# The first tile's clip and store in one piece instead of two, in a contrast adjustment on one Trainium2 core

## The chip, the cores and the metric

The kernel runs on one core of a Trainium2 chip. The core has five engines with their own instruction streams: TensorE (PE), VectorE (DVE), ScalarE (ACT), GpSimd (POOL) and SyncE (SP). Data moves between the chip's main memory and the on-chip memory (128 partitions) by DMA. A DMA is issued by an engine's queue, here SP for loads and ACT for stores, and is carried out row by row by the core's 16 DMA engines. The metric is the device time of one execution in microseconds, given as the median of several runs.

## The reference

The input is `x`, 16 x 3 images of 512 x 512 float32, and a factor of 1.5:

```python
def reference(x, factor):
    mean = np.mean(x, axis=(2, 3), keepdims=True)
    return np.clip(mean + factor * (x - mean), 0, 1).astype(np.float32)
```

Each of the 48 images needs its own mean before any of its pixels can be written. Input and output are 50.33 MB each.

## The kernel before

The 48 images are laid end to end and cut into rows of `ROW` = 8192 elements (32 KB). An image is 32 rows, so a tile of 128 partitions holds four whole images, 4 MiB, and there are 12 tiles. The on-chip buffer `ring` has `BUFS` = 6 slots of one tile each; tile t lives in slot t % 6 from its load to the end of its store, and is changed in place.

`load` (L76, issued by SP) fetches a tile or a part of its columns. At the start five loads are issued with nothing to wait for: the first 2048 columns of tile 0 (`SHORT`), its other 6144 columns, tile 1, tiles 2 and 3 in one DMA, tiles 4 and 5 in one DMA. These fill all six slots. Load t + 6 is issued after the work on tile t is written down, and waits until the store of tile t has landed, as it overwrites the same slot.

`compute(t)` sums the tile in two parts: VectorE adds up the first 4352 columns (L81) and ScalarE the other 3840 (L84, an activation that copies into `junk` and accumulates). Two small matmuls with the block matrix `blockw` (L86, L87) add the sums of the 32 rows of an image and scale them, so that `bias` (PSUM) holds (1 - factor) x mean for each row. VectorE then makes two passes over the tile: x * factor + bias (L91), and the clip to [0, 1] (L94). ACT issues the store (L101). For tile 0 alone the two passes and the store are done for 2048 columns first and then for the other 6144 (`FIRST`), so that this tile has four passes and two stores, with rows of 8 KB and of 24 KB; all other tiles have two passes and one store of 32 KB rows.

The order is written by hand: in each engine's stream the instructions of tile t stand before those of tile t + 1. So ACT's activation for tile t + 1 stands behind the store of tile t, and VectorE's sum of tile t + 1 behind the clip of tile t. Waits on semaphores are put in by the framework from what each instruction reads and writes.

Of the kernel before, what the change touches and what calls it, by code (L numbers as in the profile page):

```python
# [1 line left out]

# [4 lines left out]


P = 128  # L10
ROW = 8192
BUFS = 6
SHORT = 2048
FIRST = (SHORT, ROW - SHORT)
SUM = 4352


@with_exitstack
def kernel(
    ctx: ExitStack,  # L20
    tc: tile.TileContext,
    x: bass.AP,
    factor: float,
    out: bass.AP,
):

    nc = tc.nc
    f32 = mybir.dt.float32  # L30
    Alu = mybir.AluOpType
    Act = mybir.ActivationFunctionType

    B, C, H, W = x.shape
    n_img, n_pix = B * C, H * W
    ppi = n_pix // ROW
    per_tile = P // ppi
    n_tiles = n_img // per_tile
    assert ppi * ROW == n_pix and per_tile * n_tiles == n_img

    factor = float(factor)
    wconst = (1.0 - factor) / float(n_pix)

    x_f = x.rearrange("b c h w -> (b c h w)")
    out_f = out.rearrange("b c h w -> (b c h w)")

    def dram(ap, t, c0=0, c1=ROW):
        return bass.AP(tensor=ap.tensor, offset=t * P * ROW + c0, ap=[[ROW, P], [1, c1 - c0]])

    consts = ctx.enter_context(tc.tile_pool(name="consts", bufs=1))  # L50
    xpool = ctx.enter_context(tc.tile_pool(name="xpool", bufs=1))
    small = ctx.enter_context(tc.tile_pool(name="small", bufs=1))
    psum = ctx.enter_context(tc.tile_pool(name="psum", bufs=1, space=bass.MemoryType.PSUM))


    sums = small.tile([P, 2 * n_tiles], f32, name="sums")
    junk = small.tile([P, ROW - SUM], f32, name="junk")
    bias = psum.tile([P, n_tiles], f32, name="bias")

    blockw = consts.tile([P, P], f32, name="blockw")  # L60
    nc.gpsimd.memset(blockw, 0.0)  # L61
    for a in range(0, P, ppi):
        nc.gpsimd.memset(blockw[a : a + ppi, a : a + ppi], wconst)  # L63


    ring = xpool.tile([P, BUFS, ROW], f32, name="ring")

    def load(t, c0=0, c1=ROW, n=1):

        b = t % BUFS  # L70
        src = bass.AP(
            tensor=x_f.tensor,
            offset=t * P * ROW + c0,
            ap=[[ROW, P], [P * ROW, n], [1, c1 - c0]],
        )
        nc.sync.dma_start(out=ring[:, b : b + n, c0:c1], in_=src)  # L76

    def compute(t):
        xt = ring[:, t % BUFS, :]
        own = sums[:, 2 * t : 2 * t + 2]  # L80
        nc.vector.tensor_reduce(  # L81
            out=own[:, 0:1], in_=xt[:, 0:SUM], axis=mybir.AxisListType.X, op=Alu.add
        )
        nc.scalar.activation(out=junk, in_=xt[:, SUM:ROW], func=Act.Copy, accum_out=own[:, 1:2])  # L84
        shift = bias[:, t : t + 1]
        nc.tensor.matmul(shift, blockw, own[:, 1:2], start=True, stop=False)  # L86
        nc.tensor.matmul(shift, blockw, own[:, 0:1], start=False, stop=True)  # L87
        c = 0
        for n in FIRST if t == 0 else [ROW]:
            part = xt[:, c : c + n]  # L90
            nc.vector.tensor_scalar(  # L91
                out=part, in0=part, scalar1=factor, scalar2=shift, op0=Alu.mult, op1=Alu.add
            )
            nc.vector.tensor_scalar(  # L94
                out=part, in0=part, scalar1=0.0, scalar2=1.0, op0=Alu.max, op1=Alu.min
            )
            store(t, c, c + n)
            c += n

    def store(t, c0, c1):  # L100
        nc.scalar.dma_start(out=dram(out_f, t, c0, c1), in_=ring[:, t % BUFS, c0:c1])  # L101

    with tc.manual_schedule():
        load(0, c1=SHORT)
        load(0, c0=SHORT)
        load(1)
        load(2, n=2)
        load(4, n=2)
        for t in range(n_tiles):
            compute(t)  # L110
            if t + BUFS < n_tiles:
                load(t + BUFS)


# [1 line left out]
_INS = ['x', 'factor']  # L116
_OUTS = [((16, 3, 512, 512), 'float32')]

_NUMBERS = {'factor': 1.5}


# [26 lines left out]
```

## Time and profile before

| what | value |
|---|---|
| median of 3 runs | 239.26 us (239.2 to 239.46) |
| span of the profiled execution | 237.3 us |
| moved by DMA | 100.66 MB, mean 424 GB/s over the span |
| loads | 50.33 MB in 11 DMAs, issued by SP |
| stores | 50.33 MB in 13 DMAs, issued by ACT |
| VectorE busy | 163.1 us |
| ScalarE busy | 43.2 us |
| one sum on VectorE (L81) | 4.68 us |
| one whole-tile pass, L91 / L94 | 4.49 / 4.43 us |

The span reaches from the first to the last instruction of one profiled execution; the time of a run is some 2 us more, for what lies around it. The DMA line of the profile gives for each of 40 slices how busy the 16 DMA engines were, in tenths. A packet in the queue lists is one row of a transfer, or one of the tiny writes that signal a completion. The queue lists can be asked for any stretch of time; packets are counted in the stretch in which they begin, so that a short stretch can show more than 100%.

### The profile page before, as it was taken

How to read it: one execution, taken by the hardware profiler on the slowest of the kernel's cores; microseconds unless marked ns; L12 is line 12 of the kernel's file. 1: busy time of each engine (PE TensorE's matmuls, PEld its weight loads, DVE VectorE, ACT ScalarE, POOL GpSimd, SP SyncE). 2: the span in 40 equal slices, each digit the busy share in tenths (PEclk: the TensorE clock that was granted, in tenths of full speed). 3: DMA queues.
4: the chain of work that ended last, by engine and by line, in shares of the span. 5: the costliest groups of instructions: out<-in, count | busy, mean ns of one | idle time of the engine just before them, and what ended most of it. 6: DMA issues, size and time to landing. Idle time of an engine off the chain costs nothing.

```text
span 237.3 us, 285 instructions
## 1 busy us (share of the span) xinstructions
PE 14.1 (6%) x48; PEld 12.0 (5%) x48; DVE 163.1 (69%) x38; ACT 43.2 (18%) x25; POOL 0.9 (0%) x9
## 2 busy tenths in 40 slices
PE   0010010001010001010010100100100100010000
PEld 0010010001010001010010100100100100010000
DVE  0079989048989328999989898891892795687000
ACT  2050230041050023050320504101400500500000
POOL 1000000000000000000000000000000000000000
DMA  7999999999999999999999999999999999999996
GB/s 297 410 442 442 421 442 359 456 439 441 442 436 414 403 431 442 442 442 442 436 442 436 414 409 425 442 442 442 442 436 442 436 420 403 425 442 442 442 442 265
DMA packets 3712, 100.66 MB, mean 424 GB/s; under 512 B 384, under 2 KB 384, under 8 KB 384
## 3 DMA queue, kind: packets, MB, share of 16 engines
q1 hardware_dynamic: 1840, 50.33, 49.7%
q10 hardware_dynamic: 1872, 50.33, 49.2%
HBM read 50.33 MB, written 50.33 MB: 424 GB/s over the span
## 4 chain that ended last, share of the span: by engine, by line
DMA 57%; DVE 29%; another core or an unknown queue 3%; PE 1%; SPq 1%; issue 0%; DVEq 0%
DMA ring<-in_x_dram 41%; DMA out_dram<-ring 16%; DVE sums L81 10%; DVE ring L91 9%; DVE ring L94 9%; PE bias L87 1%; SPq L76 1%; DVEq L91 0%
## 5 line engine op out<-in xcount | busy, mean ns | idle before, releaser
L81 DVE TENSOR_REDUCE sums<-ring 128x1 f32<-128x4352 f32 x12 | 56.2, 4683 | 45.7 <-DMA ring<-in_x_dram 45.7
L84 ACT ACTIVATE junk<-ring 128x3840 f32<-128x3840 f32 x12 | 40.8, 3403 | 163.3 <-DMA ring<-in_x_dram 107.5
L91 DVE TENSOR_SCALAR ring<-ring,bias 128x8192 f32<-128x8192 f32 (+2 forms) x13 | 54.1, 4163 | 8.9 <-PE bias L87 7.4
L94 DVE TENSOR_SCALAR ring<-ring 128x8192 f32<-128x8192 f32 (+2 forms) x13 | 53.3, 4099 | 0.4
L86 PE MATMUL bias<-sums,blockw 128*128 128x1 f32 x24 | 7.0, 361 | 190.8 <-ACT junk L84 190.8
L86 PEld LDWEIGHTS bias<-sums,blockw 128*128 128x128 f32 x24 | 6.0, 312 | 191.7 <-ACT junk L84 175.2
L87 PE MATMUL bias<-sums,blockw 128*128 128x1 f32 x24 | 7.0, 363 | 4.3 <-DVE sums L81 3.9
L87 PEld LDWEIGHTS bias<-sums,blockw 128*128 128x128 f32 x24 | 6.0, 311 | 5.3 <-DVE sums L81 5.0
L84 ACT ACTIVATION_READ_ACCUMULATOR junk<-ring 128x1 f32 x12 | 2.2, 186 | 0.0
L84 ACT ACT_TABLE_LOAD x1 | 1.3, 1283 | 0.7 <-PEq L129 0.7
L63 POOL MEMSET blockw<- 32x32 f32 x4 | 0.5, 117 | 0.2
L61 POOL MEMSET blockw<- 128x128 f32 x1 | 0.2, 204 | 0.3 <-POOLq L129 0.3
L129 POOL MEMSET const-bfloat16-1.0<- 128x1 bf16 x1 | 0.1, 111 | 0.0
L129 POOL MEMSET const-uint8-127<- 128x1 uint8 x1 | 0.1, 111 | 0.0
L129 POOL MEMSET const-float32-1.0<- 128x1 f32 x1 | 0.1, 108 | 0.0
L129 POOL MEMSET const-float32-0.0<- 128x1 f32 x1 | 0.1, 103 | 0.2 <-issue 0.2
## 6 DMA issues: line engine op xcount, KB each, us to landing
out_dram<-ring ACTq DMA_DIRECT2D x11, 4096.0 KB, 35.8
ring<-in_x_dram SPq DMA_DIRECT2D x7, 4096.0 KB, 49.7
ring<-in_x_dram SPq DMA_DIRECT2D x2, 8192.0 KB, 66.7
ring<-in_x_dram SPq DMA_DIRECT2D x1, 3072.0 KB, 11.7
out_dram<-ring ACTq DMA_DIRECT2D x1, 3072.0 KB, 28.2
ring<-in_x_dram SPq DMA_DIRECT2D x1, 1024.0 KB, 4.8
out_dram<-ring ACTq DMA_DIRECT2D x1, 1024.0 KB, 17.5
```

The lines of the kernel that those rows point to most:

```text
L61: nc.gpsimd.memset(blockw, 0.0)
L63: nc.gpsimd.memset(blockw[a : a + ppi, a : a + ppi], wconst)
L76: nc.sync.dma_start(out=ring[:, b : b + n, c0:c1], in_=src)
L81: nc.vector.tensor_reduce(out=own[:, 0:1], in_=xt[:, 0:SUM], axis=mybir.AxisListType.X, op=Alu.add)
L84: nc.scalar.activation(out=junk, in_=xt[:, SUM:ROW], func=Act.Copy, accum_out=own[:, 1:2])
L86: nc.tensor.matmul(shift, blockw, own[:, 1:2], start=True, stop=False)
L87: nc.tensor.matmul(shift, blockw, own[:, 0:1], start=False, stop=True)
L91: nc.vector.tensor_scalar(out=part, in0=part, scalar1=factor, scalar2=shift, op0=Alu.mult, op1=Alu.add)
L94: nc.vector.tensor_scalar(out=part, in0=part, scalar1=0.0, scalar2=1.0, op0=Alu.max, op1=Alu.min)
L129: nc = _bacc.Bacc("TRN2", target_bir_lowering=False, num_devices=1)
```

## The change

Tile 0 is treated like every other tile: two passes over all 8192 columns, then one store. The constant `FIRST` and the loop over parts go. The loads stay as they are, the split first load included.

```diff
 SHORT = 2048
-FIRST = (SHORT, ROW - SHORT)
 SUM = 4352
...
         nc.tensor.matmul(shift, blockw, own[:, 0:1], start=False, stop=True)
-        c = 0
-        for n in FIRST if t == 0 else [ROW]:
-            part = xt[:, c : c + n]
-            nc.vector.tensor_scalar(
-                out=part, in0=part, scalar1=factor, scalar2=shift, op0=Alu.mult, op1=Alu.add
-            )
-            nc.vector.tensor_scalar(
-                out=part, in0=part, scalar1=0.0, scalar2=1.0, op0=Alu.max, op1=Alu.min
-            )
-            store(t, c, c + n)
-            c += n
+        nc.vector.tensor_scalar(
+            out=xt, in0=xt, scalar1=factor, scalar2=shift, op0=Alu.mult, op1=Alu.add
+        )
+        nc.vector.tensor_scalar(
+            out=xt, in0=xt, scalar1=0.0, scalar2=1.0, op0=Alu.max, op1=Alu.min
+        )
+        store(t, 0, ROW)
```

In the built program VectorE has two instructions fewer and ACT one store fewer; the order of everything else on every engine is the same. The completion semaphores of the DMAs, of which there are eight, are shared out in turn, so that with one DMA fewer some stores get another one.

## Prediction
> **What bounds the kernel now.** I read the page first: the engine shares, the line of 40 slices and the DMA queues.
>
> ```profile
> span 237.3 us, 285 instructions
> PE 14.1 (6%) x48; PEld 12.0 (5%) x48; DVE 163.1 (69%) x38; ACT 43.2 (18%) x25; POOL 0.9 (0%) x9
> DMA  7999999999999999999999999999999999999996
> q1 hardware_dynamic: 1840, 50.33, 49.7%
> q10 hardware_dynamic: 1872, 50.33, 49.2%
> ```
>
> No compute engine is full, and the DMA engines are full in every slice but the first and the last. Queue q1 carries the loads, q10 the stores. Their packets take 49.7 + 49.2 = 98.9% of 16 engines' span, 234.7 us of 237.3; the other 2.6 us are the start and the end. So the time is the sum of the packet times, and moving work earlier or later changes nothing unless it leaves the DMA engines idle or changes what a packet costs. The chain of waits gives DVE 29% of the span, which could mislead: transfers run all through those stretches.
>
> Next, the DMA queues of chosen stretches. The columns are packets, MB, and packet time as a share of 16 engines' time in the stretch. First the steady state, 60 to 200 us, where load rows and store rows of 32 KB alternate:
>
> ```profile
> q1 hardware_dynamic: 1039, 30.90, 51.1%
> q10 hardware_dynamic: 1025, 29.92, 49.5%
> ```
>
> 30.90 MB are 943 rows of 32,768 B (the other packets are tiny ones). 51.1% x 16 x 140 us / 943 = 1.214 us for a load row; the stores give 1.215 by the same division. Now 22 to 36 us, in which the first store (8 KB rows) starts to move, and then 36 to 46 us, in which the second store (24 KB rows) takes over:
>
> ```profile
> q1 hardware_dynamic: 148, 4.78, 81.1%
> q10 hardware_dynamic: 113, 0.93, 15.6%
> ...
> q1 hardware_dynamic: 79, 2.59, 65.1%
> q10 hardware_dynamic: 91, 1.60, 37.2%
> ```
>
> From 22 to 36 us the loads have 146 rows (4.78 MB / 32,768 B) and take 81.1% x 224 = 181.7 us, where 146 x 1.214 = 177.2 would do: 4.4 us too much over 16 engines, 0.28 us of time. From 36 to 46 us it is 79 rows and 65.1% x 160 = 104.2 us against 95.9: 8.3 us too much, 0.52 us of time. So load rows are slower than anywhere else just where the two odd stores begin, by 0.80 us together. The printed tenths of a per cent make these figures uncertain by about 0.02 us.
>
> Last, the start and the end in order of time:
>
> ```profile
> 19.65 1.23 DVE L94 TENSOR_SCALAR ring<-ring 128x2048 f32<-128x2048 f32 x1
> 20.79 3.42 DVE L91 TENSOR_SCALAR ring<-ring,bias 128x6144 f32<-128x6144 f32 x1
> 20.91 7.06 ACTq L101 DMA_DIRECT2D out_dram<-ring  x2
> 24.25 3.36 DVE L94 TENSOR_SCALAR ring<-ring 128x6144 f32<-128x6144 f32 x1
> ...
> 203.76 4.69 DVE L81 TENSOR_REDUCE sums<-ring 128x1 f32<-128x4352 f32 x1 [4.98 <-DMA ring<-in_x_dram]
> ...
> 218.17 0.34 ACTq L101 DMA_DIRECT2D out_dram<-ring  x1
> ```
>
> The first store is issued at 20.91 us; the queue's rows show none of it before 24.0 us and 16 of its packets, one per engine, from 24 to 26 us, so the lag from issue to first row is some 4 us while the loads are running (the first load of all, on idle engines, lags 1.0 us at most to its first bytes: issued at 0.74 us, 33 GB/s already in the first 2 us).
>
> **The change, part by part.** Four VectorE passes over tile 0 become two. Before: 1.29 + 1.23 + 3.42 + 3.36 = 9.30 us. After: 4.49 + 4.43 = 8.92 us by the rows of the other eleven tiles. The 0.3 to 0.4 us lie beside transfers: VectorE afterwards waits 8.77 us for tiles 2 and 3. Taken at nothing; without that cover it would be 0.4 us gained.
>
> One store issue goes (0.34 us on the ScalarE queue, in which the activation of tile 1 stands next); nothing waits for it. The store of tile 0 is issued at 18.33 + 4.53 + 4.46 = 27.3 us (one pass-to-pass distance and one pass-to-issue distance of a whole tile) instead of 20.91: 6.4 us later. Until its rows begin at about 31.3 us, the loads have the engines alone. That is no loss, since 24 MiB of loads are queued, 57 us of work at 437 GB/s.
>
> What is late next: the loads run ahead first and then give half to the store. Before, the stores have moved 4.23 MB by 56 us, as 8 KB and 24 KB rows get less than half beside 32 KB load rows. After, they move from 31.3 to 56 us at 433/2 GB/s: 5.3 MB, or 4.8 MB if the queue gives up one turn of 16 rows between two stores. So the stores are 0.6 to 1.1 MB ahead and the loads as much behind, and at half of 433 GB/s each later load lands 2.8 to 5.2 us later. Tile 0's slot comes free a few us before 55.96 us, where SyncE now issues load 6; its queue holds tiles 4 and 5 then, so it gains nothing.
>
> The end has to absorb this. From 204 us to the end the stores move 13.63 MB at 437 GB/s; the last tile is 4.19 MB or 9.6 us of it, so its rows begin near 226.0 us, 7.8 us after their issue at 218.17. Landing 2.8 to 5.2 us later leaves 2.6 to 5.0 us of cover. A lag of 1 us fits in any case, one of 4 us in most of it. Idle DMA time taken: nothing; bounds 0 and 1.4 us (4.0 - 2.6).
>
> The built program shares out the completion semaphores anew, so the stores of tiles 5, 6 and 7 also wait for loads 6, 7 and 8. Queued behind each on ScalarE is the activation of the next tile, which needs that load or a later step anyhow. Tile 7's store is the closest (issued at 144.88 us, load 8 in use at 145.73): about 1 us, with store 6 still in the queue to cover it. Nothing.
>
> What remains is the price of packets. (a) The odd rows themselves: 8 rows per engine of each kind. 15.6% x 224 us / 113 = 0.309 us for 8 KB; a 24 KB row, whose own row I take from the rate of the loads, is 0.91 us. Together 1.22 us against 1.214 for 32 KB, times 8: 0.06 us gained. (b) The 0.52 us at the takeover by the 24 KB rows: the takeover is gone, and every other one (60 to 200 us) shows load rows at 1.214. Gained 0.52; bounds 0 and 0.52. (c) The 0.28 us where stores first move: there is still a first store, with rows four times as long. No row of this trace shows 32 KB stores starting beside loads. Bounds: 0 (as at each later takeover) and 0.80 (all that the start now costs in two steps). I take 0.28 as the nearest row, so no change.
>
> The Trainium skill ("DMA: Bandwidth & Descriptors", section "Anatomy of one DMA") puts about 2 us of fixed cost on each DMA. One DMA fewer would by that give 237.3 us; the steady rows, with engines full while each completion is pending, say that this part is hidden. The same page's "Rules for kernel authors" wants transfers issued early, which speaks against the change: the 6.4 us later issue would by that cost up to 6.4 us, an estimate of 245.7 us, but here the engines are full of loads meanwhile.
>
> Sum: -0.06 - 0.52 = -0.58 us on the profiled 237.3. The median of the runs is 239.26, 2.0 us above it for what lies around the span, which stays: 238.7 us.
>
> **The rivals.** First, the loss belongs to the store stream's coming up to full share, and one start of 32 KB rows costs the whole 0.80 us. For it: both slow stretches stand at the beginning of the stores and none comes later. Against: the takeover from 24 to 32 KB rows near 55 us costs nothing. Only the 0.06 us remain: 239.2 us. Second, a clean start, as at all later takeovers: 0.06 + 0.80 = 0.86 us gained, 238.4 us. Third, on the other side, the last store comes too late: if the whole 6.4 us of delay reach the last load, its store is issued at 224.6 us, and with 4 us of lag its rows start at 228.6 instead of 226.0: 2.6 us of idle engines between the last two stores, 239.26 - 0.58 + 2.6 = 241.3 us. It decides from an issue after 222.0 us at that lag, after 225.0 us at a lag of 1 us. Against it: loads and stores share out the same bytes, so the loads fall behind only by what the stores gain.
>
> **How the numbers follow.** Forecast 0.46, first rival 0.28, second 0.12, third 0.14. This kernel's measurement can tell about 0.2% (0.48 us) from no change, so faster is below 238.78 us and slower above 239.74. The forecast lies close to the lower line: I count 0.36 of its 0.46 as faster and 0.10 as same. Faster 0.36 + 0.12 = 0.48; same 0.10 + 0.28 = 0.38; slower 0.14. The range takes in the forecast and the first two rivals, with 0.2 to 0.3 us for the spread of the three runs (0.26): 238.2 to 239.5 us.
>
> **What would show it.** The packet time of the loads between 36 and 46 us back at 1.214 us a row; an excess near 0.28 us around 31 us; the two queues' shares adding to about 98.9% of a shorter span; the last store issued between 221 and 224 us with no slice below 9 before the end. Wrong it would be if load rows stay 0.8 us too slow around 31 us, or if the DMA line dips near 225 us.

## The result, and the profile after

| | before | changed kernel |
|---|---|---|
| median of 11 runs | 239.22 us (239.04 to 239.6) | 240.3 us (239.5 to 241.89) |
| ratio | | 1.0048, 95% interval 1.0036 to 1.0059 |
| span, median of the runs | 237.4 us | 238.1 us |
| run time less span, median | 1.87 us | 2.19 us |

The changed kernel is slower by 1.08 us; 238.7 us was predicted. (The column before takes its last two rows from the runs of that kernel that stand beside the experiments. Ratios and medians of spans leave disturbed runs out.) Of the 1.08 us some 0.7 lie inside the span and 0.32 outside it. The page of one execution of the changed kernel begins like this:

```profile
span 238.0 us, 278 instructions
PE 14.0 (6%) x48; PEld 12.0 (5%) x48; DVE 162.8 (68%) x36; ACT 43.2 (18%) x25; POOL 0.9 (0%) x9
DMA  7999999999999999999999999999999999999996
q1 hardware_dynamic: 1840, 50.33, 49.6%
q10 hardware_dynamic: 1728, 50.33, 49.1%
```

The engines of the core do the same work as before, and the DMA engines are again full in every slice but the first and the last. The packets take 49.6 + 49.1 = 98.7% of 238.0 us, 234.9 us, against 234.7 before. A printed tenth of a per cent is 0.24 us here; added up packet by packet, the sum goes from 234.51 to 234.85 us. So the packets account for 0.34 us, about half of the 0.7 us by which the span grew in this execution. The timeline of the two ends shows that nothing was late in the way the third rival needed:

```profile
22.83 4.43 DVE L90 TENSOR_SCALAR ring<-ring 128x8192 f32<-128x8192 f32 x1
27.29 0.38 ACTq L96 DMA_DIRECT2D out_dram<-ring  x1
...
221.92 0.34 ACTq L96 DMA_DIRECT2D out_dram<-ring  x1
```

The first store is issued at 27.29 us and the last at 221.92, 3.75 us later than before, with some 14 us of DMA work still ahead.

The queue lists of the changed kernel, first 28 to 36 us, where its stores start to move, then 36 to 46 us (packets, MB, share of 16 engines' time):

```profile
q1 hardware_dynamic: 53, 1.74, 63.0%
q10 hardware_dynamic: 30, 0.98, 28.4%
...
q1 hardware_dynamic: 76, 2.49, 57.6%
q10 hardware_dynamic: 64, 2.10, 48.5%
```

From 28 to 36 us 53 load rows take 63.0% x 128 = 80.6 us, and 53 x 1.214 = 64.3 would do: 16.3 us too much, 1.02 us over 16 engines. From 36 to 46 us 76 rows take 92.2 us, 1.213 each, and nothing is lost. So the start of the stores alone now costs 1.02 us, where it cost 0.28 and the takeover 0.52 before.

Most of this is lost before any store row moves. From 28 to 32 us, and then from 32 to 36 us:

```profile
q1 hardware_dynamic: 33, 1.08, 83.4%
...
q10 hardware_dynamic: 30, 0.98, 56.9%
q1 hardware_dynamic: 20, 0.66, 42.6%
```

In the first four microseconds there are loads only, and their 33 rows take 83.4% x 64 = 53.4 us where 33 x 1.214 = 40.1 would do: 0.83 of the 1.02 us. The store is issued at 27.29 us and its first row begins at 32.1 us, so the slow load rows lie between the two.

That is not all. The same list from 140 to 190 us, store queue only, first before, then after:

```profile
q10 hardware_dynamic: 377, 11.31, 52.4%
```

```profile
q10 hardware_dynamic: 381, 10.91, 50.9%
```

Before, 11.31 MB are 345 rows of 32,768 B, and 52.4% x 800 us / 345 is 1.215 us. After, 10.91 MB are 333 rows at 1.223 us. A small loss, but from the single packets it lies on ten of the 16 engines, up to 0.43 us on one between 100 and 200 us. And the engines end apart. From 235.5 us on, before and after:

```profile
q10 hardware_dynamic: 15, 0.00, 0.4%
```

```profile
q10 hardware_dynamic: 17, 0.03, 4.2%
```

Before, only completions are left; after, a whole row still begins. By the packets the engines end between 235.47 and 236.05 us before, and between 235.65 and 236.75 us after. The span follows the last of the 16, not their mean: it is 1.2 us longer than the last end in both. The mean of the 16 ends rose by 0.36 us (235.67 to 236.03), the last end by 0.7. The last engine of the changed kernel lost 0.27 us in slow rows after 60 us; without them it would end at 236.48 us, still 0.43 us after the last one before. So in this execution the larger part comes from the start.

### The profile page after: what moved, and what is told of

Read it like the earlier page. It is cut to its first block, busy times and chain, and to the rows that moved or that the text cites. A ratio compares the mean times of both kernels' runs of the same rounds, so it can differ in the third digit from the quotient of the medians.

```text
span 238.0 us, 278 instructions
## 1 busy us (share of the span) xinstructions
PE 14.0 (6%) x48; PEld 12.0 (5%) x48; DVE 162.8 (68%) x36; ACT 43.2 (18%) x25; POOL 0.9 (0%) x9
## 3 DMA queue, kind: packets, MB, share of 16 engines
q1 hardware_dynamic: 1840, 50.33, 49.6%
q10 hardware_dynamic: 1728, 50.33, 49.1%
## 5 line engine op out<-in xcount | busy, mean ns | idle before, releaser
L87 DVE TENSOR_SCALAR ring<-ring,bias 128x8192 f32<-128x8192 f32 x12 | 53.9, 4492 | 8.9 <-PE bias L86 7.5
L90 DVE TENSOR_SCALAR ring<-ring 128x8192 f32<-128x8192 f32 x12 | 53.1, 4427 | 0.4
```

What stands on the lines that cost most here:

```text
L87: nc.vector.tensor_scalar(out=xt, in0=xt, scalar1=factor, scalar2=shift, op0=Alu.mult, op1=Alu.add)
L90: nc.vector.tensor_scalar(out=xt, in0=xt, scalar1=0.0, scalar2=1.0, op0=Alu.max, op1=Alu.min)
```

## The experiments

Three theories stood at the beginning. Theory 1: the loads stall where the rows of the store stream begin or grow, and long first rows cost more. Theory 2: the 6.4 us later start costs. Theory 3: the number of store DMAs counts. Theory 4 came out of the first four runs. The offset that it speaks of is how long after a load tile's first row a store tile's first row begins, taken from the packets' start times (the median over the 16 engines, at the store of tile 4); both streams repeat every 19.4 us. Offsets and packet times come from the one execution of each kernel that was profiled, medians of spans from all its runs.

**late_two_stores.** Whole passes, but two stores:

```diff
-        store(t, 0, ROW)
+        c = 0
+        for n in (SHORT, ROW - SHORT) if t == 0 else [ROW]:
+            store(t, c, c + n)
+            c += n
```

> Two whole passes over tile 0 as in the changed kernel, and behind them two stores as in the kernel before: 8 KB rows, then 24 KB rows, both issued at about 27.3 us. Theory 1 (loads stall where the rows of the store stream begin or grow, the more the longer the new row): the loads' excess is 0.28 + 0.52 = 0.8 us again, only later, in place of 1.02 us in the changed kernel, no row is slow from 100 to 200 us, and the time is 239.2 to 239.4 us. Theory 2 (the 6.4 us later start of the stores costs): 240.3 us as in the changed kernel. Theory 3 (the number of store DMAs counts, not their rows): 239.2 us.

Measured 240.19 us, ratio 1.0034 (1.0024 to 1.0043). Theory 3 falls: the stores are as many as before and as long, and the time is near the changed kernel's. Theory 1 is not enough: the loads' excess between 20 and 60 us is 0.93 us against 0.88 before, by the packets. But rows between 100 and 160 us are slow, 0.11 us in the mean and up to 0.33 us on single engines, which theory 1 did not expect.

**early_passes_one_store.** Four passes, one store:

```diff
-            store(t, c, c + n)
             c += n
+        store(t, 0, ROW)
```

> Four passes over tile 0 as before, and one store of 32 KB rows behind them, issued at about 27.6 us. All three theories expect the time of the changed kernel, 240.0 to 240.5 us, with about 1 us of excess in the loads near 30 us; if the passes themselves mattered it would be 239.2 us.

Measured 241.11 us, ratio 1.0071 (1.0048 to 1.0094): as slow as the changed kernel or slower. The passes are not the cause.

**late_half_partitions.** Two stores of 64 partitions:

```diff
-        store(t, 0, ROW)
+        if t == 0:
+            for p in (0, P // 2):
+                half = bass.AP(tensor=out_f.tensor, offset=p * ROW, ap=[[ROW, P // 2], [1, ROW]])
+                nc.scalar.dma_start(out=half, in_=ring[p : p + P // 2, 0, :])
+        else:
+            store(t, 0, ROW)
```

> As the changed kernel, but tile 0 is stored in two DMAs of 64 partitions each, both with rows of 32 KB. Theory 1 (row length at the start): 240.3 us, about 1 us of excess near 30 us. Theory 2 (late start): 240.3 us. Theory 3 (number of store DMAs): 239.2 us.

Measured 245.94 us, ratio 1.0279. No theory expected this. By the packets 2.05 us of excess lie between 60 and 200 us, where the kernel before has 0.01, and the engines end between 238.3 and 242.5 us. Its offset is 2.7 us.

**two_halves_16k.**

```diff
-FIRST = (SHORT, ROW - SHORT)
+FIRST = (4096, 4096)
```

> The kernel before with the parts of tile 0 at 4096 and 4096 columns: first store rows of 16 KB, issued at about 23 us, and then no growth until the 32 KB rows of tile 1. Theory 1: 0.5 us of excess in the loads at the start (half of 1.02), 0 to 0.5 us where the 32 KB rows take over, so 239.0 to 239.5 us. Theory 2 (cost by the start's delay, 1.08 us for 6.4 us): the start is some 2.2 us later than before, 239.6 us. Theory 3: 239.2 us.

Measured 239.22 us, ratio 1.0 (0.9991 to 1.0008). The excess is 0.81 us, as before (0.88), though the rows start at 16 KB: what the start costs in all depends little on how the first store is cut. That a start 2 us later costs nothing speaks against theory 2.

In these runs and the two kernels of the study, slow late rows went with an offset of 1.2 us (changed kernel, late_two_stores, early_passes_one_store) or 2.7 us, and none were seen at 9.7 us (before) and 12.1 us (two_halves_16k). This is theory 4.

**later_store.** The store of tile 0 written behind ScalarE's activation of tile 1:

```diff
         nc.scalar.activation(out=junk, in_=xt[:, SUM:ROW], func=Act.Copy, accum_out=own[:, 1:2])
+        if t == 1:
+            store(0, 0, ROW)
+            load(BUFS)
...
-        store(t, 0, ROW)
+        if t:
+            store(t, 0, ROW)
...
-            if t + BUFS < n_tiles:
+            if t and t + BUFS < n_tiles:
                 load(t + BUFS)
```

> As the changed kernel, but the store of tile 0 stands behind the activation of tile 1 on ScalarE's queue, so it is issued some 4 us later still, at about 31.2 us, and so is load 6. Theory 2 (a late start of the stores costs, 1.08 us for 6.4 us): 0.7 us more than the changed kernel, 241 us. Theory 4 (it costs when the tiles of the load stream and of the store stream begin together: a store tile begins 9.7 us after a load tile in the kernel before, 12.1 us with two 16 KB halves, but 1.2 us in the changed kernel and 1.2 us with two late stores): the loads move 4 us ahead and the stores 4 us back, the offset becomes 9 us, and the time 239.2 to 239.6 us. Theory 1 (row length at the start alone): 240.3 us, like the changed kernel.

Measured 240.07 us, ratio 1.0036 (1.0023 to 1.005). The edit missed: tile 1 had landed early, the activation ran ahead of the clip of tile 0, and the store was issued at 27.28 us as before the edit, with the offset at 1.2 us. It counts only as the changed kernel once more.

**offset_moved_from_after, offset_moved_from_before, offset_by_a_tile.** A tiny extra load between two others, with 48 rows (112 in the third):

```diff
         load(2, n=2)
+        extra = small.tile([48, 64], f32, name="extra")
+        nc.sync.dma_start(out=extra, in_=bass.AP(tensor=x_f.tensor, offset=0, ap=[[ROW, 48], [1, 64]]))
```

> The changed kernel with one more load between those of tiles 2 and 3 and of tiles 4 and 5: 48 rows of 256 B into a small tile that nothing reads. It moves 12 KB, but takes four turns of the load queue on each engine (three rows and the completion), so that from some 50 us on the loads stand four rows, 9.7 us, further back against the stores. Offset 10.9 instead of 1.2 us. Theory 4: 239.2 to 239.6 us. Theories 1 and 2: 240.3 us.

> The kernel before with the same extra load of 48 rows of 256 B at the same place. Offset 0.0 instead of 9.7 us, with the stores still starting early and in 8 KB rows. Theory 4: as slow as the changed kernel, 240.0 to 240.5 us, with slow rows on some engines from 60 us on. Theories 1 and 2: 239.2 to 239.3 us.

> The changed kernel with an extra load of 112 rows of 256 B at that place: eight turns, so the loads stand a whole tile further back and the offset is again 1.2 us. It has the same extra DMA and the same semaphores as the run with 48 rows. Theory 4: 240.3 us, like the changed kernel. If the extra DMA helped by itself, or through the semaphores, it would be 239.2 to 239.6 us.

Ratios 1.0039 (1.0016 to 1.0061), 1.0034 (1.0017 to 1.005) and 1.0041 (1.0011 to 1.0071). Inconclusive: tiny rows don't take a turn each, all three ended near an offset of 18.3 us and not where they were meant to, and the times scattered, from 239.46 to 253.44 us in the first. In the third, 7 of the 12 runs took 248.6 to 251.5 us, which its ratio does not count; its profiled execution, one of these, has offsets of 18.2 to 19.6 us and 1.33 us of excess after 60 us. So the offset alone does not tell the time. A small DMA over part of the partitions is no clean way to shift a stream.

**later_still.** VectorE's sum of tile 1 between the two passes over tile 0, by which the store really moves (to 31.83 us):

```diff
-            compute(t)
+            if t != 1:
+                total(t)
+            scale(t)
+            if t == 0:
+                total(1)
+            clip(t)
```

(`total`, `scale` and `clip` are the three parts of `compute`; the store stands in `clip`.)

> As the changed kernel, but VectorE's sum of tile 1 stands between the two passes over tile 0, so that the whole store of tile 0 (32 KB rows) is issued at about 32.0 instead of 27.3 us; no instruction more or less. Its first rows move near 37 us. Theory 2 (a late start of the stores costs): 241.0 us or more. Theory 4 (it costs when tiles of the load stream and of the store stream begin together): the offset goes from 1.2 to about 10.6 us, as in the kernel before, and the time to 239.2 to 239.5 us. Theory 1 (long rows at the start): 240.3 us, like the changed kernel.

Measured 240.08 us, ratio 1.0036 (1.0024 to 1.0048); median span 237.6 us. The run time seems to refute theory 4 (offset now 9.6 us). But the run time less the span is 2.40 us here, against 1.87 in the kernel before, so only 0.2 of the 0.8 us are inside the span, where DMA rows can count. No row after 60 us is slow: the excess there is 0.01 us. Theory 2 falls: 4.5 us later, and the span is no longer than the changed kernel's (0.5 us shorter by the medians).

**later_still_two_stores.** The same, with the two stores of late_two_stores.

> The same order, with the store of tile 0 as two DMAs of 8 KB and 24 KB rows, issued at about 32.0 us. Theory 2: 240.9 us or more. Theory 4: offset near 10.6 us, 239.2 to 239.4 us. Theory 1: 239.2 to 239.4 us. With the two stores issued at 27.3 us (offset 1.2 us) it was 240.19 us.

Measured 239.79 us, ratio 1.0027 (1.0016 to 1.0038); span 237.4 us, the same as before, offset 9.7 us; the rest, 2.44 us, is outside. With that the four kernels make a square (median spans of 5 to 12 runs):

| median span, us | offset 9.6 to 9.7 us | offset 1.2 us |
|---|---|---|
| two stores of tile 0 | 237.4 (later_still_two_stores) | 237.85 (late_two_stores) |
| one store | 237.6 (later_still) | 238.1 (changed kernel) |

By these medians the offset is worth 0.45 to 0.5 us and the single store some 0.2. But the single runs overlap: 237.2 to 238.2 and 237.2 to 238.1 us with two stores, 237.6 to 238.0 and 237.3 to 239.7 us with one. The traces divide the difference otherwise. In later_still the last engine ends at 236.55 us, 0.5 us after the last one before, and only 0.05 us of that lies in slow rows after 60 us; the changed kernel's last engine ends at 236.75 us. So the square points to the offset but does not price it.

**parts_6144_2048.**

```diff
-FIRST = (SHORT, ROW - SHORT)
+FIRST = (ROW - SHORT, SHORT)
```

> The kernel before with the parts of tile 0 at 6144 and 2048 columns: 24 KB rows first, issued near 25.1 us, first rows some 4 us later. Theory 1: 0.75 us of excess at the start and more where 8 KB rows give way to 32 KB rows; 239.4 to 239.9 us. Theory 2: 4.2 us later than before, 0.7 us, 240.0 us. Theory 4: the offset of 9.7 us grows by twice the 4 us or so, to 17 to 18.5 of 19.4 us, so that load tiles begin 1 to 2.5 us after store tiles: between 239.3 and 240.3 us, the slower the closer.

Measured 239.29 us, ratio 1.0002 (0.9994 to 1.0011), offset 16.9 us: as fast as before, with 24 KB rows first and a start 4 us later. Theories 1 and 2, as they were priced, expected more; theory 4 holds only at the lower edge of its range. Load tiles that begin 2.5 us after store tiles cost nothing.

**four_parts.**

```diff
-FIRST = (SHORT, ROW - SHORT)
+FIRST = (1024, 1024, 2048, 4096)
```

> The kernel before with tile 0 in four parts of 1024, 1024, 2048 and 4096 columns, so that the rows of the first stores grow from 4 to 4, 8, 16 and then 32 KB, beginning about 1 us earlier than before. Theory 1: less excess at each step; if only the steps up to 24 KB cost, as before, the sum is 0.5 to 0.9 us, and the time 239.0 to 239.4 us. Theories 2 and 4 (early start; offset 5 to 15 us): 239.0 to 239.4 us.

Measured 240.62 us, ratio 1.0053 (1.0036 to 1.007), with spans in two groups, at 237.3 and from 238.2 to 238.7 us. All theories missed this. The profiled execution is one of the good ones and has 0.80 us of excess at the start; what the others lose stays open. With an offset of 12.1 us theory 4 has no place for a median span of 238.45 us.

**start_two_sums and start_two_sums_plus.** The first pass over tile 1 goes ahead of the clip of tile 0 too; in the second kernel, shown here, so does an idle sum (the `tensor_reduce`), which brings the offset past a full period:

```diff
-            compute(t)
+            if t > 1:
+                total(t)
+                scale(t)
+            if t == 0:
+                total(0)
+                scale(0)
+                total(1)
+                scale(1)
+                nc.vector.tensor_reduce(
+                    out=spare, in_=ring[:, 1, 0:1024], axis=mybir.AxisListType.X, op=Alu.add
+                )
             clip(t)
```

> As the run later_still, with the first pass over tile 1 moved ahead of the clip of tile 0 as well: the whole store of tile 0 is issued at about 36.5 instead of 32.0 us. Theory 4 (what counts inside the span is the offset of store tiles behind load tiles, with a period of 19.4 us): the offset grows from 9.8 by some 8 to 9 us to near 18 us, that is 1 to 1.5 us short of a full period; span between 237.6 us (as at 16.9 us in the kernel with parts of 6144 and 2048) and 238.1 us (as at 1.2 us). Theory 2 (late start): span 238.0 us or more. Theory 1: 237.6 us, as in later_still.

> The same with one more VectorE sum over 1024 columns that nothing uses, about 1.1 us, ahead of the clip of tile 0: store issued at about 37.6 us, offset some 2 us further, near 20 = 0.6 us. Theory 4: median span 238.0 to 238.2 us, as in the changed kernel at 1.2 us. Theory 1: 237.6 us, as in later_still. Theory 2: more than in start_two_sums.

Measured 239.9 us, ratio 1.0026 (1.0014 to 1.0038), span 237.7 us at an offset of 18.2; and 242.7 us, ratio 1.0137 (1.0123 to 1.0151), span 240.15 us at 2.5. The queue lists from 100 to 190 us, start_two_sums and then start_two_sums_plus:

```profile
q10 hardware_dynamic: 675, 19.50, 50.2%
q1 hardware_dynamic: 671, 19.40, 50.0%
```

```profile
q1 hardware_dynamic: 664, 19.66, 51.9%
q10 hardware_dynamic: 655, 18.84, 48.6%
```

A load row takes 50.0% x 1440 us / 592 = 1.216 us in the first and 51.9% x 1440 / 600 = 1.246 us in the second. The mean hides that the slow rows come in bursts, one in each period. The loads of the second kernel from 104.5 to 117.5 us, and then from 178 to 186 us:

```profile
q1 hardware_dynamic: 80, 2.62, 46.7%
...
q1 hardware_dynamic: 62, 2.00, 62.5%
```

That is 46.7% x 208 us / 80 = 1.214 us for a row in the first stretch and 62.5% x 128 / 61 = 1.311 us in the second, where the store of one tile gives way to the next. Two thirds of what the load rows lose between 60 and 200 us falls on the second row of a load tile (12.3 of 18.8 us over the 16 engines). The first store is issued only 1.15 us later (38.39 against 37.24 us), and the span is 2.45 us longer. Theory 2 has no place for that, nor theory 1; theory 4 has the direction but expected 238.0 to 238.2. The offset of 2.5 us is dearer than 1.2 us, and so it is in late_half_partitions at 2.7 us.

**after_padded and before_padded.** Three idle instructions behind all the work:

```diff
                 load(t + BUFS)
+        for i in range(2):
+            nc.vector.memset(spare[:, i : i + 1], 0.0)
+        nc.scalar.activation(out=spare[:, 2:3], in_=sums[:, 0:1], func=Act.Copy)
```

> The changed kernel with two memsets of one column on VectorE and one activation of one column on ScalarE behind all the work, in the shade of the last store. Every transfer is as in the changed kernel: median span 238.1 us. If the time outside the span belongs to the program's layout it moves by 0.1 us or more from 2.19 us; if it belongs to the transfers it stays.

> The kernel before with the same three idle instructions: span 237.4 us. Outside the span: moves by 0.1 us or more from 1.87 us if it belongs to the layout, stays if it belongs to the transfers.

Run time less span went from 2.19 to 1.97 us in the changed kernel, and from 1.87 to 2.06 us in the kernel before (single runs of before_padded 1.84 to 2.19). It moved by 0.2 us each, in opposite directions, with every transfer in its place. So it belongs to the program and not to its DMAs; what in the program stays open. The spans: 237.35 us for before_padded, and 238.8 us (238.3 to 239.3, four runs) for after_padded, above the 238.1 expected. The runs of the changed kernel itself go from 237.3 to 239.7 us, so two kernels with the same transfers differ here by as much as the change made.

All kernels but those with the extra load, in the order of the offset; the excess is what all rows of 4 KB and more took beyond the time of their bytes at the steady rate of 32 KB rows, per engine (the own price of the short rows, some 0.07 us in most kernels that have them and 0.16 in four_parts, is in it):

| kernel | first rows KB | offset us | excess 20 to 60 us | excess 60 to 200 us | median span | run less span |
|---|---|---|---|---|---|---|
| changed kernel | 32 | 1.2 | 1.02 | 0.19 | 238.1 | 2.19 |
| late_two_stores | 8 | 1.2 | 0.93 | 0.12 | 237.85 | 2.42 |
| early_passes_one_store | 32 | 1.2 | 1.02 | 0.19 | 238.55 | 2.56 |
| later_store | 32 | 1.2 | 1.30 | 0.25 | 237.8 | 2.29 |
| after_padded | 32 | 1.2 | 0.92 | 0.47 | 238.8 | 1.97 |
| start_two_sums_plus | 32 | 2.5 | 0.80 | 1.37 | 240.15 | 2.56 |
| late_half_partitions | 32 | 2.7 | 3.38 | 2.05 | 243.6 | 2.30 |
| before_padded | 8 | 9.4 | 0.92 | 0.15 | 237.35 | 2.06 |
| later_still | 32 | 9.6 | 0.93 | 0.01 | 237.6 | 2.40 |
| later_still_two_stores | 8 | 9.7 | 0.84 | 0.01 | 237.4 | 2.44 |
| before | 8 | 9.7 | 0.88 | 0.01 | 237.4 | 1.87 |
| two_halves_16k | 16 | 12.1 | 0.81 | 0.01 | 237.3 | 2.02 |
| four_parts | 4 | 12.1 | 0.80 | 0.07 | 238.45 | 2.18 |
| parts_6144_2048 | 24 | 16.9 | 0.94 | 0.01 | 237.4 | 1.94 |
| start_two_sums | 32 | 18.2 | 1.21 | 0.09 | 237.7 | 2.19 |

For theory 4 speaks that all kernels with an offset of 1.2 to 2.7 us have a median span of 237.8 us or more, and all others one of 237.7 us or less, but for four_parts. Against it as the whole cause speaks, besides four_parts, that an offset of 1.2 us slows rows only for part of the time: in the changed kernel it holds from 72 us on, but of the 44 rows above 1.225 us between 60 and 200 us 33 begin from 148 to 172 us.

## Why the prediction was wrong

**What bounds the kernel.** Right: the DMA engines are full to the end in both kernels. But from it I drew that the time is the sum of the packet times. In the traces that sum rose by 0.34 us and the span by 0.7, as the span follows the slowest of 16 engines. I never asked how far apart they end.

**Passes and issues.** Right. The store is issued at 27.29 us (27.3 forecast), the last one at 221.92 us (221 to 224 forecast), with no idle engines; the third rival did not occur. The first store rows begin at 32.1 us, 0.8 us later than forecast, with loads still queued. One store DMA fewer saved nothing either: later_still has one fewer than later_still_two_stores, and its median span is 237.6 against 237.4 us. The section that the prediction quotes for 2 us per DMA describes DMAs issued from GpSimd; these come from SP and ACT.

**(b) and (c), the step that failed.** "The takeover is gone ... Gained 0.52." The takeover is gone, and rows from 36 to 46 us are back at 1.213 us. But (c), "I take 0.28 as the nearest row, so no change", is wrong by 0.74 us: the start now costs 1.02 us, above even the bound of 0.80. Together the loads' excess went from 0.80 us to 1.02, a loss of 0.22 where I forecast a gain of 0.52. The first rival came closest: coming up to full share costs about the same in one step or two. The other cuts of the first store agree: 0.80 to 0.94 us with first rows of 4, 8, 16 and 24 KB. With 32 KB rows it was 0.80 to 1.30 us, so that the loss of 0.22 is within what single executions differ by; that the forecast gain did not come is clear. But the first rival's 239.2 us missed too, by 1.1 us. Term (a) held: the single rows take 0.309 + 0.912 = 1.221 us against 1.213.

**The term that was missing.** The sum has no entry for how the two streams lie against each other. I worked out that the stores would be 0.6 to 1.1 MB ahead and the loads as much behind, and used it only for the end. That same shift brought the tiles of both streams to begin 1.2 instead of 9.7 us apart. In the profiled execution rows after 60 us then took 0.19 us too long per engine, against 0.01 before; the square above would give the offset 0.45 to 0.5 us of span, without being clear of the scatter. That lateness is not the cause, start_two_sums and start_two_sums_plus show (2.45 us of span for 1.15 us). That the offset is, they make likely and four_parts and the runs with the extra load leave in doubt; why rows slow down at such an offset was not tried.

**Around the span.** "2.0 us above it for what lies around the span, which stays" did not hold: it is 0.32 us more by the medians, and the 11 runs lie close together (2.12 to 2.21 us). Three idle instructions move this part by 0.2 us.

Of the measured 1.08 us, 0.32 lie outside the span. How the 0.7 us inside divide is open: the medians of the square give about 0.5 to the offset and 0.2 to the single store, the two traces 0.43 to the start and 0.27 to slow rows later on.

## What to carry to other kernels

Where two streams of equal rows fill the DMA engines, a change at the start sets how they lie against each other for the whole run: compare the last end of the 16 engines, and the offset of the streams, not just the sum of the packets. A loss seen at one step of a ramp need not vanish with the step; it may move to the one that is left. And compare spans and run times separately before explaining a few tenths of a microsecond: a part outside the span moves with instructions that do nothing.

## What was not expected of the hardware

A start of the stores beside running loads slowed the loads by 0.8 to 1.3 us per engine in all kernels with stores over 128 partitions, whatever the rows of the first store, and in the changed kernel 0.83 of the 1.02 us were lost before the first store row began. Where the tiles of the two streams begin 1.2 us apart, some store rows are slow for part of the time (1.223 against 1.215 us in the mean from 140 to 190 us). At 2.5 us apart load rows took 1.246 instead of 1.216 us in the mean, in bursts once a tile, and the span was 2.45 us longer; in the sole kernel with a store over 64 partitions (2.7 us apart) it was 6.2 us longer than before. In the kernels of the table at 9.4 to 18.2 us the profiled executions have at most 0.15 us of excess after 60 us, and 0.01 in most. Time outside the span differed by up to 0.7 us (1.87 to 2.56 us) among kernels that differ in a few instructions.
